# Strassen's seven products for 12 of 32 channel blocks in the two ways out of a retention and pooling trunk

## The chip, the core and the metric

The kernel runs on one core of one Trainium2 chip. The metric is the device time of one execution in microseconds. The engines named below are TensorE (PE, whose weight loads are PEld), VectorE (DVE), ScalarE (ACT), GpSimd (POOL) and SyncE (SP, which issues most of the loads); PSUM is the memory of eight banks into which PE adds its products, each bank 128 partitions by 512 values of fp32.

## What is computed

A trunk of two layers over 256 tokens and 2048 channels. The first is a retention layer of eight heads, the second a gated pooling over four windows; each has a wide way in, its own core, and a way out of 4096 channels back to 2048, which is added to the stream. A last norm ends it.

```python
def retention_layer(x, g_norm, w_in, gn, w_out):
    h = rms_norm(x, g_norm)
    ...
    o = chunkwise_retention(q, k, v)
    ...
    o = o.astype(x.dtype) * jax.nn.silu(z)      # (1, 256, 4096)
    return o @ w_out                            # w_out (4096, 2048)

def pooling_layer(x, g_norm, w_in, w_grp, b_grp, scale, w_out):
    ...
    mix = mix.reshape(B, S, POOL_WIDTH) * scale
    return (mix * jax.nn.silu(z)) @ w_out       # (1, 256, 4096) @ (4096, 2048)

def reference(x, ...):
    h = x
    h = h + retention_layer(h, ...)
    h = h + pooling_layer(h, ...)
    return rms_norm(h, final_norm)
```

## The kernel before

Everything is fp32. A value that goes through PE is held as a pair in the type fp32r: hi, which ACT makes as a cast (`split`, L69), and lo, which DVE makes by subtracting hi from the value (L70). A product of two such pairs is three matmuls: hi by hi, hi by lo, lo by hi.

Weights stream from memory in units of 1 MB, 128 rows by 2048, which SP loads into a ring of three buffers `raw`. `weights` splits each in two halves of 1024 columns into `whi` and `wlo`, three buffers each. So ACT and DVE handle each unit in two instructions of 1024 each, and a `raw` buffer is free again when DVE has done the second.

The way out of layer 1 multiplies `os` (the 256 tokens by 4096 channels, as 32 blocks of 128 channels, each a pair) with `ret_out`. It goes through four column blocks of 512. For each there are two sums in PSUM (`accr`, one for each half of 128 tokens) and eight units; a unit holds four channel blocks of these 512 columns, and each channel block gives three matmuls of 512 columns for each half of the tokens (`row_product`, L334 to L336): 24 matmuls to a unit, 768 in all. Behind each column block DVE adds the two sums to the stream `xn` (L358), ACT squares it for the next norm (L360), and PE transposes it in pieces of 128x128 into `turned` (L366). From there ACT and DVE make `hs2` (`split_scaled`, L74 and L75), the left side of the pool's way in, whose first products are `stationary` (L98, L99). All 16 channel blocks of `hs2` are needed there.

The way out of layer 2 does the same with `gs`, `pool_out` and `accy`, without transposes. In its last column block the last two units are held back, and then done for the first half of the tokens and after that for the second, in an order written by hand (`manual_schedule`), so that the norm of the first half runs while PE does the second. The last unit's pairs have a place of their own, `own`. DVE adds (L478), ACT squares (L480), POOL multiplies by the gain `gb`, DVE works out the root, and the rows are scaled and stored.

What stands ahead of the ways out also counts: `os` is complete when the last head's normalization has gone through its root steps (`rsqrt`, L123 to L139, on `rs_t` and `ors`), its products with the gate `gz` (L322, L325) and a split (L327) into the last four blocks. `gs` is complete behind the last steps of the pool's groups (from L437 on).

A list scheduler orders the instructions of each engine at build time, by a simulated timeline, except where the program asks for its own order. Each engine then works through its list strictly in that order.

## Time and profile before

| | |
|---|---|
| time, median of 3 runs | 1390.14 us (1389.86 to 1391.74) |
| profiled execution, its own time | 1390.88 us |
| span of its trace | 1388.7 us |
| PE busy in the span | 1373.2 us |
| DVE / ACT busy in the span | 958.1 / 681.8 us |
| layer 1's way out, from its first product to its last | 579.4 to 756.4 us |
| layer 2's way out | 1204.6 to 1379.2 us |

Times in the trace are microseconds from the start of the span. The three runs give the time that counts; the profiled execution is one more run, and its trace is what can be read, so a forecast built from rows is first a forecast of 1390.88. A matmul's record is longer than its share of the engine, since matmuls overlap: what one costs where they follow each other is the distance between starts. The tables by stretch give for each stretch its length, then busy time and instructions of PE, PEld, DVE, ACT and POOL, the clock granted to PE as a share of full speed, the share of the DMA engines' time, and GB/s. In a row of a group by line, "out<-in" names what is written and read, with partitions by elements.

### The profile page before, as it was taken

To read this page: it belongs to the slowest core of one execution; us is meant where nothing else is said; L and a number is where in the kernel's file an instruction comes from. 1 tells how busy PE (TensorE), PEld (TensorE's weight loads), DVE (VectorE), ACT (ScalarE), POOL (GpSimd) and SP (SyncE) were. 2 spreads that over 40 slices of the span, in tenths; PEclk is the share of its full clock that TensorE was granted. 3 is DMA by queue.
4 is the path that set the end of the run, shared out by engine and by line. 5 is a ranking of instruction groups with operands and counts; after the bars stand their busy time and mean duration, and the time that the engine had idled before them with its cause. 6 is when DMAs were issued, how large, how long until landed. Compare 5 with 4: busy or idle time off the path is not lost.

```text
span 1388.7 us, 18364 instructions
## 1 busy us (share of the span) xinstructions
PE 1373.2 (99%) x7224; PEld 1177.2 (85%) x7224; DVE 958.1 (69%) x1398; ACT 681.8 (49%) x975; POOL 24.5 (2%) x33
## 2 busy tenths in 40 slices
PE   8999999999999999999999999999999999999997
PEld 7888888888888888888888888888888888888885
DVE  6886868686868676754555767876885896744454
ACT  6554555454545454544444445545454545544443
POOL 0000000000000000000000000000000000000001
PEclk9999999999999999999999999999999999999999
DMA  7545454555554545575555555555555555555552
GB/s 295 182 168 207 165 192 168 187 180 187 181 189 164 185 170 183 180 252 197 191 182 189 180 196 192 188 186 186 195 199 182 185 194 197 210 189 205 184 194 109
DMA packets 39493, 262.66 MB, mean 189 GB/s; under 512 B 4512, under 2 KB 4896, under 8 KB 9072
## 3 DMA queue, kind: packets, MB, share of 16 engines
q1 hardware_dynamic: 37872, 255.93, 52.4%
q0 software_dynamic: 1536, 5.57, 1.1%
q8 instruction: 56, 0.92, 0.3%
q14 instruction: 29, 0.24, 0.0%
HBM read 259.39 MB, written 2.10 MB: 188 GB/s over the span
## 4 chain that ended last, share of the span: by engine, by line
PE 98%; DVE 1%; DMA 1%; ACT 0%; issue 0%; SPq 0%; DVEq 0%; ACTq 0%
PE acc L98 37%; PE acc L99 19%; PE accv L278 4%; PE accv L280 4%; PE accy L334 4%; PE accv L279 4%; PE accr L335 4%; PE accr L336 4%; PE accr L334 4%; PE accy L335 4%; PE accy L336 4%; PE po L298 1%; PE acc L197 1%; DMA xin<-in_xT 1%; PE po L300 1%; PE sc L252 0%
## 5 line engine op out<-in xcount | busy, mean ns | idle before, releaser
L70 DVE TENSOR_TENSOR wlo<-raw,whi 128x1024 fp32r<-128x1024 f32 x470 | 575.3, 1224 | 375.7 <-ACT whi L69 372.6
L69 ACT CAST whi<-raw 128x1024 fp32r<-128x1024 f32 x470 | 494.7, 1053 | 642.4 <-PE acc L98 297.8
L98 PE MATMUL acc<-hs,whi 128*128 128x512 f32 x1984 | 697.3, 395 | 0.0
L99 PE MATMUL acc<-hs,wlo 128*128 128x256 f32 x1984 | 556.3, 281 | 0.0
L98 PEld LDWEIGHTS acc<-hs,whi 128*128 128x128 f32 x1984 | 371.9, 188 | 85.3
L99 PEld LDWEIGHTS acc<-hs,wlo 128*128 128x128 f32 x1984 | 374.9, 189 | 1.1
L335 PE MATMUL accr<-wlo,os 128*128 128x512 f32 x256 | 99.9, 390 | 0.0
L280 PE MATMUL accv<-whi,hs 128*128 128x512 f32 x256 | 99.9, 390 | 0.0
L279 PE MATMUL accv<-wlo,hs 128*128 128x512 f32 x256 | 99.8, 390 | 0.0
L336 PE MATMUL accr<-whi,os 128*128 128x512 f32 x256 | 99.7, 389 | 0.0
L335 PE MATMUL accy<-wlo,gs 128*128 128x512 f32 x248 | 96.5, 389 | 0.0
L336 PE MATMUL accy<-whi,gs 128*128 128x512 f32 x248 | 96.5, 389 | 0.0
L278 PE MATMUL accv<-whi,hs 128*128 128x512 f32 x256 | 92.1, 391 | 0.9 <-DVE qk L108 0.9
L334 PE MATMUL accr<-whi,os 128*128 128x512 f32 x256 | 91.2, 390 | 0.0
L98 PE MATMUL acc<-ms,whi 128*128 128x512 f32 x256 | 90.6, 397 | 0.0
L334 PE MATMUL accy<-whi,gs 128*128 128x512 f32 x248 | 88.1, 389 | 0.0
L99 PE MATMUL acc<-ms,wlo 128*128 128x256 f32 x256 | 72.0, 281 | 0.0
L98 PEld LDWEIGHTS acc<-ms,whi 128*128 128x128 f32 x256 | 48.0, 188 | 11.8
L278 PEld LDWEIGHTS accv<-whi,hs 128*128 128x128 f32 x256 | 48.1, 188 | 11.3 <-DVE qk L108 1.2
L334 PEld LDWEIGHTS accr<-whi,os 128*128 128x128 f32 x256 | 48.1, 188 | 10.0
L336 PEld LDWEIGHTS accr<-whi,os 128*128 128x128 f32 x256 | 48.1, 188 | 9.9
L335 PEld LDWEIGHTS accr<-wlo,os 128*128 128x128 f32 x256 | 48.1, 188 | 9.8
(150 smaller groups left out, 1141.9 us busy)
## 6 DMA issues: line engine op xcount, KB each, us to landing
raw<-in_ret_in SPq DMA_DIRECT2D x92, 1024.0 KB, 4.8
raw<-in_pool_in SPq DMA_DIRECT2D x64, 1024.0 KB, 4.9
raw<-in_ret_out SPq DMA_DIRECT2D x32, 1024.0 KB, 4.9
raw<-in_pool_out SPq DMA_DIRECT2D x32, 1024.0 KB, 4.9
raw<-in_pool_grp SPq DMA_DIRECT2D x16, 1024.0 KB, 4.9
xin<-in_ret_in SPq DMA_DIRECT2D x7, 512.0 KB, 8.3
xn<-in_xN POOLq DMA_DIRECT2D x4, 512.0 KB, 9.3
out<-xn SPq DMA_DIRECT2D x8, 256.0 KB, 2.3
```

Of the source, the lines that this page charges most:

```text
L69: nc.scalar.copy(hi, src)
L70: nc.vector.tensor_tensor(out=lo, in0=src, in1=hi.bitcast(F32), op=ALU.subtract)
L98: nc.tensor.matmul(acc, hi, moving[:, k], start=(k == 0), stop=False)
L99: nc.tensor.matmul(acc[:, :S], lo, moving[:, k, 0], start=False, stop=(k == n - 1))
L197: nc.tensor.matmul(accs[c], hi[:, b], hs[:, k], start=(k == 0), stop=False)
L278: nc.tensor.matmul(accv[t], hs[:, k, 0, ts], hi[:, ws], start=(k == 0), stop=False)
L279: nc.tensor.matmul(accv[t], hs[:, k, 0, ts], lo[:, ws], start=False, stop=False)
L280: nc.tensor.matmul(accv[t], hs[:, k, 1, ts], hi[:, ws], start=False, stop=(k == KT - 1))
L298: nc.tensor.matmul(po[:, :S], vs[:, 0, p, cs], ss[:, q, :S], start=(n == 0), stop=(n == 2))
L334: nc.tensor.matmul(acc, A[:, k, 0, ts], hi, start=first, stop=False)
L335: nc.tensor.matmul(acc, A[:, k, 0, ts], lo, start=False, stop=False)
L336: nc.tensor.matmul(acc, A[:, k, 1, ts], hi, start=False, stop=last)
```

## The change

Strassen's scheme multiplies two 2x2 arrangements of blocks with seven products instead of eight, at the price of sums of blocks ahead of the products and behind them. Here an arrangement is: two halves of 128 tokens by two channel blocks of 128 on the left, two channel blocks by two column blocks of 512 on the right. Of the 32 channel blocks the first 20 go on as before (units "C"), the last 12 form six pairs, block j with block j + 6 (units "S", still 1 MB: two channel blocks by two column blocks). The column blocks are done in two pairs, and a pair of column blocks has 16 units in the order CCCSCSCSCSCSCSCC.

For each pair there are eight sums in PSUM: four of results (c11, c21, c12, c22, by half of the tokens and column block), and p1, p5, p6, p7 for products that go into more than one result. They take all eight banks, so the pools of banks are opened and closed by stage. An S unit needs on DVE three sums of weights (`s0` of 1024, `s1` in two of 512) and the splits of these and of the plain parts: 3.5 times 1024. The left side needs four forms of sums of token blocks, made once for each layer from the last 12 blocks by `sides`: one sum of 128x3072, four of 128x768, four splits. The seven products of an S unit are 21 matmuls. Behind the sixth S, DVE puts p1, p5, p6, p7 and the results together in nine sums out of PSUM (some by way of `u`). The pairs of weights now share one tile `w` with four buffers, hi and lo together; one of four buffers `u0` to `u3` of the pool is dropped, and the weights are laid out in memory in the new order.

```diff
+ORDER = "CCCSCSCSCSCSCSCC"
+NS = ORDER.count("S")
+CLASSIC = ((0, 0), (0, 1), (1, 0), (1, 1), (2, 0), (2, 1), (3, 0), (4, 0), (3, 1), (4, 1))
...
+    def load(src):
         raw = wpool.tile([P, UNIT], F32, tag="raw", name="raw", bufs=3)
         nc.sync.dma_start(out=raw, in_=src)
+        return raw
+    def pair_of(src, n):
+        w = wpool.tile([P, 2, HALF], F32R, tag="w", name="w", bufs=4)
+        hi, lo = w[:, 0, :n], w[:, 1, :n]
+        split(hi, lo, src)
+        return hi, lo
+    def weights(src, own=None):
+        raw = load(src)
         halves = []
         for i in range(2):
+            half = raw[:, i * HALF : (i + 1) * HALF]
             if own is None:
-                hi = wpool.tile([P, HALF], F32R, tag="whi", name="whi")
-                lo = wpool.tile([P, HALF], F32R, tag="wlo", name="wlo")
+                halves.append(pair_of(half, HALF))
             else:
-                hi, lo = own[:, i, 0], own[:, i, 1]
-            split(hi, lo, raw[:, i * HALF : (i + 1) * HALF])
-            halves.append((hi, lo))
+                split(own[:, i, 0], own[:, i, 1], half)
+                halves.append((own[:, i, 0], own[:, i, 1]))
         return halves
...
+    class Sum:
+        def __init__(self, pool, name, n):
+            self.tile, self.n, self.done = pool.tile([P, 512], F32, tag=name, name=name), n, 0
+        def add(self, a_hi, a_lo, w_hi, w_lo):
+            for a, w in ((a_hi, w_hi), (a_hi, w_lo), (a_lo, w_hi)):
+                nc.tensor.matmul(self.tile, a, w, start=(self.done == 0), stop=(self.done == self.n - 1))
+                self.done += 1
+    def sides(A, tmp, pieces):
+        a = tmp[:, : 2 * NS * S].rearrange("p (k s) -> p k s", s=S)
+        s = tmp[:, 2 * NS * S : 2 * NS * S + NS * P].rearrange("p (k s) -> p k s", s=P)
+        blocks = A[:, VT - 2 * NS :]
+        nc.vector.tensor_tensor(out=a, in0=blocks[:, :, 0].bitcast(F32), in1=blocks[:, :, 1].bitcast(F32), op=ALU.add)
+        a11, a21, a12, a22 = a[:, :NS, :P], a[:, :NS, P:], a[:, NS:, :P], a[:, NS:, P:]
+        def put(form, src):
+            for dst, j, n in pieces:
+                split(dst[:, :n, form, 0], dst[:, :n, form, 1], src[:, j : j + n])
+        nc.vector.tensor_tensor(out=s, in0=a21, in1=a22, op=ALU.subtract)
+        put(0, s)
+        nc.vector.tensor_tensor(out=a21, in0=a11, in1=a21, op=ALU.subtract)
+        put(2, a21)
+        nc.vector.tensor_tensor(out=s, in0=s, in1=a11, op=ALU.subtract)
+        put(1, s)
+        nc.vector.tensor_tensor(out=s, in0=s, in1=a12, op=ALU.add)
+        put(3, s)
+        forms = []
+        for dst, j, n in pieces:
+            forms += [[(dst[:, i, m, 0], dst[:, i, m, 1]) for m in range(4)] for i in range(n)]
+        return forms
...
+    def way_out(A, src, forms, pool, order, y, after, own=None):
+        def blk(k, t):
+            ts = slice(t * P, (t + 1) * P)
+            return A[:, k, 0, ts], A[:, k, 1, ts]
+        for p in range(2):
+            plain = sum(1 for k, c in CLASSIC if c == 0) * 12
+            sums = {}
+            for name in order:
+                n = 0 if name == "c22" else 3 * NS
+                sums[name] = Sum(pool, name, n + (plain if name[0] == "c" else 0))
+            out_of = {(t, c): sums[f"c{t + 1}{c + 1}"] for t in range(2) for c in range(2)}
+            classic, strassen, held = iter(CLASSIC), 0, []
+            def add(t, c, op, in1):
+                o = y(t, 2 * p + c)
+                nc.vector.tensor_tensor(out=o, in0=o, in1=in1, op=op)
+            def rows(unit, t):
+                (k4, c), halves = unit
+                for i, (hi, lo) in enumerate(halves):
+                    for j in range(2):
+                        ws = slice(j * 512, (j + 1) * 512)
+                        out_of[t, c].add(*blk(4 * k4 + 2 * i + j, t), hi[:, ws], lo[:, ws])
+            for n, kind in enumerate(ORDER):
+                unit = src[p * len(ORDER) + n]
+                if kind == "C":
+                    last = own is not None and p == 1 and n >= len(ORDER) - 2
+                    u = (next(classic), weights(unit, own if last and n == len(ORDER) - 1 else None))
+                    if last:
+                        held.append(u)
+                    else:
+                        rows(u, 0)
+                        rows(u, 1)
+                    continue
+                raw = load(unit)
+                b = raw.rearrange("p (m f) -> p m f", m=4)
+                s = [wpool.tile([P, 2, 512], F32, tag=f"s{i}", name=f"s{i}", bufs=1) for i in range(2)]
+                nc.vector.tensor_tensor(out=s[0], in0=b[:, 1:3], in1=b[:, None, 0].broadcast_to([P, 2, 512]), op=ALU.add)
+                b_hi, b_lo = pair_of(raw[:, 512:1536], 1024)
+                nc.vector.tensor_tensor(out=s[1][:, 0], in0=s[0][:, 0], in1=b[:, 2], op=ALU.add)
+                nc.vector.tensor_tensor(out=s[1][:, 1], in0=s[1][:, 0], in1=b[:, 3], op=ALU.add)
+                b21 = pair_of(raw[:, 1536:], 512)
+                t_pairs = [pair_of(x.rearrange("p m f -> p (m f)"), 1024) for x in s]
+                def cut(pair, i):
+                    return pair[0][:, i * 512 : (i + 1) * 512], pair[1][:, i * 512 : (i + 1) * 512]
+                k1 = VT - 2 * NS + strassen
+                k2 = k1 + NS
+                s1, s2, s3, s4 = forms[strassen]
+                strassen += 1
+                sums["p1"].add(*blk(k1, 0), *cut((b_hi, b_lo), 0))
+                sums["c12"].add(*s4, *cut((b_hi, b_lo), 1))
+                sums["c11"].add(*blk(k2, 0), *b21)
+                sums["p5"].add(*s1, *cut(t_pairs[0], 0))
+                sums["p7"].add(*s3, *cut(t_pairs[0], 1))
+                sums["p6"].add(*s2, *cut(t_pairs[1], 0))
+                sums["c21"].add(*blk(k2, 1), *cut(t_pairs[1], 1))
+                if strassen == NS:
+                    u = ev.tile([P, 512], F32, tag="u", name="u", bufs=1)
+                    nc.scalar.copy(u, sums["p1"].tile)
+                    add(0, 0, ALU.add, sums["c11"].tile)
+                    add(0, 0, ALU.add, u)
+                    after(0, 2 * p)
+                    nc.vector.tensor_tensor(out=u, in0=u, in1=sums["p6"].tile, op=ALU.add)
+                    add(0, 1, ALU.subtract, u)
+                    add(1, 0, ALU.add, sums["c21"].tile)
+                    nc.vector.tensor_tensor(out=u, in0=u, in1=sums["p7"].tile, op=ALU.add)
+                    add(1, 0, ALU.add, u)
+                    after(1, 2 * p)
+                    add(0, 1, ALU.add, sums["p5"].tile)
+                    add(1, 1, ALU.add, sums["p5"].tile)
+                    add(1, 1, ALU.subtract, u)
+            if held:
+                with tc.manual_schedule(engines={mybir.EngineType.PE}):
+                    for t in range(2):
+                        for u in held:
+                            rows(u, t)
+            for t in range(2):
+                add(t, 1, ALU.add, out_of[t, 1].tile)
+                after(t, 2 * p + 1)
...
+        with tc.tile_pool(name="way1", bufs=1, space=bass.MemoryType.PSUM) as way:
+            tmp = act.tile([P, 2 * NS * S + NS * P], F32, tag="hs", name="tmp")
+            big = pl.tile([P, 4, 4, 2, P], F32R, tag="ms", name="forms")
+            small = pl.tile([P, NS - 4, 4, 2, P], F32R, tag="gz", name="forms")
+            forms = sides(os, tmp, ((big, 0, 4), (small, 4, NS - 4)))
+            hs2 = act.tile([P, KT, 2, S], F32R, tag="hs", name="hs2")
...
+            way_out(os, ret_out, forms, way, ("p1", "p5", "p6", "p7", "c11", "c21", "c12", "c22"), stream, turn)
+        second = ctx.enter_context(ExitStack())
+        second.enter_context(banks("second"))
...
+        with tc.tile_pool(name="way2", bufs=1, space=bass.MemoryType.PSUM) as way:
+            tmp = pl.tile([P, 2 * NS * S + NS * P], F32, tag="ms", name="tmp")
+            forms = act.tile([P, NS, 4, 2, P], F32R, tag="hs", name="forms")
+            forms = sides(gs, tmp, ((forms, 0, NS),))
+            own = pl.tile([P, 2, 2, HALF], F32R, tag="ms", name="own")
+            way_out(gs, pool_out, forms, way, ("p1", "p5", "p6", "c11", "c21", "c12", "c22", "p7"), stream, norm, own)
...
+    def mixed_units(w):
+        w = w.reshape(VT, P, 4, 512)
+        units = []
+        for c in (0, 2):
+            classic, j = iter(CLASSIC), VT - 2 * NS
+            for kind in ORDER:
+                if kind == "C":
+                    k4, i = next(classic)
+                    units.append(w[4 * k4 : 4 * k4 + 4, :, c + i])
+                else:
+                    units.append(np.stack([w[j, :, c + 1], w[j, :, c], w[j + NS, :, c + 1], w[j + NS, :, c]]))
+                    j += 1
+        return np.stack(units).transpose(0, 2, 1, 3).reshape(-1, P, UNIT)
...
-    nc = bacc.Bacc("TRN2", target_bir_lowering=False, num_devices=1)
+    nc = bacc.Bacc("TRN2", target_bir_lowering=False, num_devices=1, dynamic_dma_scratch_size=2048)
```

How this stands in the lists of two engines is shown at three places.

**Layer 1's way out begins, DVE.** Before, the last head's products with the gate `gz` and the split into `os` stand among the subtractions of weights (`wlo`), and nothing else follows from them on this engine:

```order
L322 TENSOR_TENSOR gz_4973<-gz_4973,ors_4952 128x1024
L70 TENSOR_TENSOR wlo_5258<-raw_5251,whi_5257 128x1024
L325 SCALAR_TENSOR_TENSOR gz_4973<-o_4915,vec_73,gz_4973 128x256 x4
L70 TENSOR_TENSOR wlo_5288<-raw_5285,whi_5287 128x1024
L70 TENSOR_TENSOR os_365<-gz_4973,os_365 128x4x256
L70 TENSOR_TENSOR wlo_5292<-raw_5285,whi_5291 128x1024
```

In the changed program the same steps have the subtractions for the first S (`w` from `raw`, from `s0`) between them, and the sum of 3072 behind them:

```order
L346 SCALAR_TENSOR_TENSOR gz_4789<-o_4731,vec_67,gz_4789 128x256 x4
L81 TENSOR_TENSOR w_5135<-raw_5125,w_5135 128x512
L81 TENSOR_TENSOR os_357<-gz_4789,os_357 128x4x256
L81 TENSOR_TENSOR w_5138<-s0_5127,w_5138 128x1024
L369 TENSOR_TENSOR tmp_4996<-os_357 128x3072
```

A few rows on, the first forms stand behind the last split of the first S, the weight sums of the second (`s0`, `s1`) and a plain unit's subtraction; the other forms follow still later:

```order
L81 TENSOR_TENSOR w_5141<-s1_5128,w_5141 128x1024
L433 TENSOR_TENSOR s0_5199<-raw_5197 128x1024
L81 TENSOR_TENSOR w_5167<-raw_5165,w_5167 128x1024
L376 TENSOR_TENSOR tmp_4996<-tmp_4996 128x768
L435 TENSOR_TENSOR s1_5200<-s0_5199,raw_5197 128x512
L378 TENSOR_TENSOR tmp_4996<-tmp_4996 128x6x128
L436 TENSOR_TENSOR s1_5200<-s1_5200,raw_5197 128x512
L81 TENSOR_TENSOR forms_4997<-tmp_4996,forms_4997 128x4x128
L81 TENSOR_TENSOR forms_4998<-tmp_4996,forms_4998 128x2x128
```

What moved: between `os` and the first product that needs a form there is now a list of sums and splits on DVE, with the weights of two S units and of C units among them.

**Layer 1's way out ends, PE.** Before, the pool's products (L98, L99 into `acc`) follow the last product of the way out, and the last transposes come later among them:

```order
L334 MATMUL accr_6079<-whi_6324,os_365 128x512
L335 MATMUL accr_6079<-wlo_6325,os_365 128x512
L336 MATMUL accr_6079<-whi_6324,os_365 128x512
L98 MATMUL acc_6429<-hs2_5178,whi_6421 128x512
L99 MATMUL acc_6429<-hs2_5178,wlo_6422 128x256
L98 MATMUL acc_6429<-hs2_5178,whi_6421 128x512
```

In the changed program, where `turned` has a bank for each quarter and the pool's banks come free with the way out's, the transposes of both last column blocks stand between:

```order
L360 MATMUL c22_5654<-w_6222,os_357 128x512
L360 MATMUL c12_5653<-w_6222,os_357 128x512 x5
L360 MATMUL c22_5654<-w_6222,os_357 128x512 x5
L510 MATMUL turned_6173<-idt_303,xn_4987 128x128
L510 MATMUL turned_6164<-idt_303,xn_4987 128x128 x3
L510 MATMUL turned_6173<-idt_303,xn_4987 128x128 x3
L510 MATMUL turned_6255<-idt_303,xn_4987 128x128
L510 MATMUL turned_6264<-idt_303,xn_4987 128x128
L510 MATMUL turned_6255<-idt_303,xn_4987 128x128 x3
L510 MATMUL turned_6264<-idt_303,xn_4987 128x128 x3
L119 MATMUL acc_6329<-hs2_5020,w_6323 128x512
L120 MATMUL acc_6329<-hs2_5020,w_6323 128x256
```

What moved: the pool's first product (L119, L120) now stands behind 16 transposes, and these behind the sums into `xn`.

**Layer 2's way out ends, DVE.** Before, the subtractions of the last two units stand one after the other, and the first sum out of PSUM comes behind them all:

```order
L70 TENSOR_TENSOR wlo_11674<-raw_11667,whi_11673 128x1024
L70 TENSOR_TENSOR own_10642<-raw_11711,own_10642 128x1024 x2
L70 TENSOR_TENSOR wlo_11704<-raw_11701,whi_11703 128x1024
L70 TENSOR_TENSOR wlo_11708<-raw_11701,whi_11707 128x1024
L478 TENSOR_TENSOR xn_5177<-xn_5177,accy_11495 128x512
L491 TENSOR_SCALAR rs_a_11772<-part_10643,base_10644 128x1
```

In the changed program the two subtractions into `own` and two sums into `xn` stand around the last subtraction of the last S (`w` from `s1`), ahead of the last C but one (`w` from `raw`):

```order
L81 TENSOR_TENSOR w_11478<-s0_11467,w_11478 128x1024
L81 TENSOR_TENSOR own_10406<-raw_11535,own_10406 128x1024
L409 TENSOR_TENSOR xn_4987<-xn_4987,c11_11004 128x512
L81 TENSOR_TENSOR own_10406<-raw_11535,own_10406 128x1024
L81 TENSOR_TENSOR w_11481<-s1_11468,w_11481 128x1024
L409 TENSOR_TENSOR xn_4987<-xn_4987,u_11505 128x512
L81 TENSOR_TENSOR w_11529<-raw_11527,w_11529 128x1024
L81 TENSOR_TENSOR w_11532<-raw_11527,w_11532 128x1024
```

What moved: the first sum out of PSUM, which needs c11 complete, now stands ahead of three subtractions of weights.

## Rows read from the trace of the kernel before

**Rows 1.** Page, part 1 (busy us, share, instructions); the chain by engine

```profile
PE 1373.2 (99%) x7224; PEld 1177.2 (85%) x7224; DVE 958.1 (69%) x1398; ACT 681.8 (49%) x975; POOL 24.5 (2%) x33
...
PE 98%; DVE 1%; DMA 1%; ACT 0%; issue 0%; SPq 0%; DVEq 0%; ACTq 0%
```

**Rows 2.** Waits of PE: who waited <- for whom: us, times, longest

```profile
PE acc L197 <- ACT whi L69: 4.0, 3, 2.4
PE cold L162 <- POOL ones_f L156: 1.0, 1, 1.0
PE accv L278 <- DVE qk L108: 0.9, 1, 0.9
```

**Rows 3.** Both ways out: stretch, busy us (x instructions) by engine, clock, DMA

```profile
579.40:756.40 177.00, 177.00 (x794) 146.54 (x793) 94.90 (x107) 77.77 (x91) 3.39 (x5) 1.00 0.57 203
...
1204.60:1379.20 174.60, 174.52 (x770) 144.04 (x768) 85.18 (x90) 72.64 (x82) 11.74 (x8) 1.00 0.51 175
```

**Rows 4.** Layer 1's sums: duration ns min/median/max, first and last start

```profile
L334 PE MATMUL accr<-whi,os x256: 389/389/476, 579.4 to 755.8; 128*128 128x512 f32 x128
...
L336 PE MATMUL accr<-whi,os x256: 387/389/398, 579.9 to 756.2; 128*128 128x512 f32 x128
```

**Rows 5.** The chain that ended last: start us, us, what

```profile
760.93 0.66 PE turned L366 x6
```

**Rows 6.** DVE in order of time, head 7's end: start us, us, instruction

```profile
579.97 0.43 DVE L138 SCALAR_TENSOR_TENSOR rs_t<-rs_t,rs_a 128x256 f32<-128x256 f32 x1
...
583.52 1.23 DVE L70 TENSOR_TENSOR wlo<-raw,whi 128x1024 fp32r<-128x1024 f32 x1
584.66 0.42 DVE L139 SCALAR_TENSOR_TENSOR ors<-rs_t,ors 128x256 f32<-128x256 f32 x1
585.11 0.42 DVE L137 TENSOR_TENSOR rs_t<-ors 128x256 f32<-128x256 f32 x1
...
592.89 1.23 DVE L70 TENSOR_TENSOR os<-gz,os 128x1024 fp32r<-128x1024 f32 x1
```

**Rows 7.** Groups by line: count, busy us, mean ns, idle before it

```profile
L69 ACT CAST whi<-raw 128x1024 fp32r<-128x1024 f32 x470 | 494.7, 1053 | 642.4 <-PE acc L98 297.8 <-PE accr L336 97.1 <-PE accy L336 88.5
...
L75 DVE SCALAR_TENSOR_TENSOR hs<-turned,vec,hs 128x256 fp32r<-128x256 f32 x16 | 7.1, 477 | 0.1
...
L74 ACT ACTIVATE hs<-turned,vec 128x256 fp32r<-128x256 f32 x16 | 6.8, 471 | 1.7 <-PE turned L366 1.5 <-DVE hs L75 0.2
...
L358 DVE TENSOR_TENSOR xn<-xn,accr 128x512 f32<-128x512 f32 x8 | 5.1, 680 | 0.0
```

**Rows 8.** Instructions of line 210, durations in ns

```profile
L210 DVE TENSOR_TENSOR xin<-xin x3: 685/1218/2293, 28.7 to 34.3; 128x2048 f32<-128x2048 f32 x1, 128x1024 f32<-128x1024 f32 x1, 128x512 f32<-128x512 f32 x1
```

**Rows 9.** DMA issues: count, KB each, median us from issue to landing

```profile
raw<-in_ret_out SPq DMA_DIRECT2D x32, 1024.0 KB, 4.9
```

**Rows 10.** DVE in order of time, layer 2's way out begins

```profile
1204.56 0.48 DVE L437 SCALAR_TENSOR_TENSOR m<-acc,vec,hl 128x256 f32<-128x256 f32 x1
```

**Rows 11.** PE in order of time, layer 1's last product and the next

```profile
756.21 0.39 PE L336 MATMUL accr<-whi,os 128*128 128x512 f32 x1
...
756.44 0.39 PE L98 MATMUL acc<-hs,whi 128*128 128x512 f32 x1
```

**Rows 12.** In order of time, PE's last matmul

```profile
1378.72 0.40 PE L336 MATMUL accy<-own,gs 128*128 128x512 f32 x1
```

**Rows 13.** Stretches at the start and the end, columns as in rows 3

```profile
8.00:10.00 2.00, 1.74 (x7) 1.26 (x5) 0.49 (x1) 0.40 (x2) 0.00 (x0) 0.50 1.00 370
...
14.00:16.00 2.00, 1.64 (x7) 1.11 (x8) 1.71 (x3) 2.00 (x5) 0.00 (x0) 0.96 1.03 400
...
1379.20:1381.20 2.00, 0.00 (x0) 0.00 (x0) 1.08 (x4) 0.98 (x3) 0.46 (x1) 1.00 1.02 384
...
1383.20:1385.20 2.00, 0.00 (x0) 0.00 (x0) 1.20 (x3) 0.57 (x1) 0.00 (x0) 0.50 0.36 137
```

186 lines of the change are left out of this document (79 added, 107 removed).

## The prediction

> **What bounds the kernel now.** I read the engines' totals first, then the chain that ended last, the waits, the stages, and last single rows of the two ways out. PE is busy 99% of the span, and 98% of the chain is PE's [rows 1]. It waits for other engines 4.0 + 1.0 + 0.9 us in all, at the start [rows 2]. In the two ways out (579.4 to 756.4 and 1204.6 to 1379.2 us) PE is busy to within 0.1 us, DVE 54% and 49%, ACT 44% and 42% [rows 3]. So each product taken away is worth its whole pitch, as long as every product left finds its operands ready. In layer 1's way out 768 products start between 579.4 and 756.2 [rows 4], with 24 transposes of 0.11 (six take 0.66 us [rows 5]) among them: (176.8 - 2.6) / 767 = 0.227 us each.
>
> **What it removes.** 12 of 32 blocks are six pairs; per pair and half of the columns seven products of three matmuls stand where there were eight: 3 matmuls less, 6 x 2 x 2 x 3 = 72 in all. 72 x 0.227 = **16.3 us less**. Loads stay at 1 MB per unit.
>
> **What it adds, in the steady part.** A Strassen unit (S) brings DVE two sums of 1024 in width (three instructions) and 3.5 subtractions of 1024 where a plain unit (C) has two. A row of 1024 at 583.52 takes 1.23 us, and the next starts at 584.66: 1.14 after it [rows 6]; with the same overlap 0.68 at 512 [rows 7] gives 0.60, and 0.42 at 256 gives 0.34, while rows of 256 that need the row ahead stand 0.45 apart [rows 6]. From 2293 ns at 2048 and 1218 at 1024 [rows 8], 768 takes 0.87 and 3072 3.3 us. A pair S + C then costs DVE 3.5 x 1.14 + 2 x 1.14 + 2.34 = 8.6 us and PE (21 + 24) x 0.227 = 10.2. ACT has 5.5 casts of 1.05 [rows 7]: 5.8. All of it lies beside PE, and I cost it at nothing. One loop is tight: a raw block is loaded when the second subtraction of the C ahead ends, 4.9 us from issue to landing [rows 9]; then the sum, the last subtraction of the S under way, the next C's two and half a sum (4 x 1.14 + 0.6) must pass until it is free again: about 10.1 against 10.2. After an entry (below) the operands of the next C are some 2.6 us early, so I take 0 here, and at most 4 us in all if two loads meet and land 0.5 us later.
>
> **The entry of layer 1.** S reads four forms made from the last 12 blocks of os, and the last four blocks are written by head 7's end, 592.89 + 1.23 in the rows [rows 6]. PE meanwhile has three C, and the changed order lets it draw C4 ahead: 72 + 24 + 21 = 117 matmuls, 26.6 us, from 579.4 to 606.0. DVE must in the same time get from the first S's sum to the fourth form. I carry its queue in the changed order. The head's first root step stands at 579.97 + 0.43 [rows 6]; in the changed order two rows of the last gate block (0.34 each) and a wait for its copy come ahead of it: 581.4. The raw block for the sum lands at 581.6 (its buffer is free once C1's second half is subtracted, by the same carry 576.6, plus 4.9). Up to the first piece of the fourth form stand 12 rows of 1024 (13.7 us), 9 of 512 (5.4), 14 of 256 (5.3), 4 of 768 (3.5), one of 3072 (3.3), memsets (0.3): 31.5 us. Three waits for ACT's casts come to 1.8: the os cast, one for the cast of C4's second half (whose pair comes free only when PE has done the third form's products) and the fourth form's. 581.6 + 31.5 + 1.8 = 614.9, visible at 615.1. Behind it PE has one matmul and 12 more of C4: 618.1. **Loss 12.1 us.** DVE is then 85% loaded, PE is the bound again, and nothing gives this back.
>
> **The entry of layer 2.** The same with 120 matmuls (1204.6 + 27.2 = 1231.8). DVE is at the last but one block's bias step at 1204.56 [rows 10]; 12 rows of 1024 (13.7), 5 of 512 (3.0), 8 of 768 (7.0), 3.3, and the pool's last six steps (2.7) end at 1234.4; 13 matmuls follow: 1237.4. **Loss 5.6 us**; it is smaller because no head's end stands in the queue.
>
> Here a rule can be weighed. The two rows at 583.52 and 584.66 overlap by 0.09 us [rows 6]. The Trainium skill ("VectorE: DVE Perf Modes", Terms) says that a pipeline flush follows every DVE operation and that the next can't issue until the pipe is empty; by that, without any overlap, some 70 rows would add about 6 us to the two losses. The row decides, and I use the pitches.
>
> **The turn between the layers.** Before, PE goes on at 756.44 with the pool's products, 0.23 us after the last one [rows 11], and turns the last columns among them. In the changed order all 16 transposes stand ahead of the pool's first product, and on DVE the last sum (c22) stands behind a split of the third column's turned block. From the last product: 0.8 (seven transposes), ACT 0.47, DVE 0.48, the sum 0.68 [rows 7], six transposes 0.66, with releases 3.35 us, where 15 transposes alone take 1.65. **Loss 1.7 us.**
>
> **The end of layer 2.** Ahead of the last S's fourth subtraction stand own's two and the first sum out of PSUM, which waits for c11. From the end of the C before: c11 visible at 1.75 (7 matmuls and 0.16), sum 2.35, own 3.5, subtraction done 4.7; PE is there after 16 matmuls, 3.6. Then a sum (0.6) and 1.14 stand ahead of the next half: 6.4 against 5.7. **Loss 1.9 us.** The nine sums out of PSUM that follow end 4 us before PE does, so the 9.6 us from the end of PE's last matmul (1378.72 + 0.40 [rows 12]) to the end of the span stay.
>
> **The clock.** In layer 1's entry PE has from about 597.4 to 602.3 one matmul, and up to 614.4 works a third of the time. After PE's last matmul the granted clock is 1.00 from 1379.2 to 1381.2 and 0.50 (1.2 GHz) from 1383.2 to 1385.2; at the start it is 0.50 from 8 to 10, with PE 87% busy, and 0.96 from 14 to 16 [rows 13]. A fall can cost nothing (DVE is the bound there), or half of some 6 us once PE runs free: 0 to 3. I take 2, nearer to the rows of the start.
>
> **Sum.** -16.3 + 12.1 + 5.6 + 1.7 + 1.9 + 2.0 = +7.0. The profiled execution took 1390.88 (span 1388.7 and 2.2 around it): 1397.9. The median of three is 0.74 lower: **1397 us, slower**.
>
> **Rivals.**
> The entries are hidden. Half of the subtractions and sums for the first S need weights only; were they done beside the head's last products, the forms would come earlier. For: DVE is 54% busy over the way out before [rows 3]. Against: only four pairs of buffers, and in the queue the head's root steps stand among them. With both entries hidden: 1390.1 - 16.3 + 3.6 = 1377; with half of the losses, 1386 to 1390. It decides for faster once the four losses together are under 13.5 us.
> More waits than counted. The raw block's loop above (up to 4), and the clock. The Trainium skill ("TensorE: Matmul & The Clock Gate", Part 1) says that the throttled state is the default and that activity releases it. By that, where the rows only show that idling to the end brings 0.50, the thin activity of the entry could already do so; the price in rows is the whole 3. Time: 1399 to 1404. For: the loop has 0.1 us of room. Against: margins after the entries.
> That the change doesn't do what it says I give nothing: the built program has 72 matmuls less.
>
> **How the numbers follow.** About 0.2% (2.8 us) is what a measurement here can tell from no change. Forecast, 1393 to 1399: 0.55. More waits: 0.2. Entries half hidden, 1387 to 1393: 0.13; hidden further, below 1387: 0.12. So faster 0.12, same 0.13, slower 0.75. The range 1387 to 1403 leaves out the hidden entries and the far end of the waits.
>
> **What would show it.** After: PE waiting in layer 1's way out about 12 us, nearly all in its first 40, for DVE's subtractions of forms and weights; about 5.6 in layer 2's first 35; 1 to 2 at the turn, for xn; 2 in the last 25 us; none in between; 72 matmuls less at 0.227. DVE near 95% in the entries and 85% after. A granted clock under 1 between 600 and 622 shows the clock's term. I am wrong if PE waits under 8 us in layer 1's way out, or if S + C pairs take more than 10.3 us.

## The result, and the profile after

| | before | after |
|---|---|---|
| time, median | 1390.06 us (1389.86 to 1391.74, 4 runs) | 1401.51 us (1401.20 to 1403.37, 4 runs) |
| profiled execution, span | 1390.88, 1388.7 us | 1403.37, 1401.4 us |
| ratio of the runs | | 1.0082, interval 1.0065 to 1.0100 |

The change makes the kernel 11.4 us slower. The forecast was 1397, within 1387 to 1403: direction and range held, and the loss was 1.6 times the 7.0 of the sum. The traced execution of after is the slowest of its four, 1.9 us above the median; its first head's products start at 36.25 us, in the trace of before at 35.38.

The page of after, as in [rows 1]: instructions and busy time of the engines, and the chain by engine. PE has 72 matmuls less, DVE is busy 143 us more, and PE's share of the chain falls from 98% to 92%.

```profile
PE 1367.8 (98%) x7152; PEld 1167.2 (83%) x7152; DVE 1101.6 (79%) x1571; ACT 735.4 (52%) x1039; POOL 24.4 (2%) x33
...
PE 92%; DVE 4%; DMA 2%; ACT 1%; issue 1%; SPq 0%; DVEq 0%; ACTq 0%
```

The waits of PE, as in [rows 2] (who waited <- for whom: us, times, longest). None of these six was there before.

```profile
PE c L360 <- DVE w L81: 4.6, 3, 2.6
...
PE acc L119 <- DVE rs_t L158: 3.0, 1, 3.0
PE c L360 <- ACT w L80: 2.7, 3, 1.2
PE turned L510 <- DVE xn L409: 2.6, 2, 2.3
...
PE c L360 <- DVE m L585: 1.0, 1, 1.0
...
PE c L360 <- DVE gz L129: 0.9, 1, 0.9
```

The stretches, with the columns of [rows 3]: the first 41 us of layer 1's way out and the rest of it, then the same for layer 2.

```profile
576.90:618.00 41.10, 34.15 (x129) 24.98 (x130) 37.33 (x54) 17.96 (x24) 3.40 (x5) 0.92 0.52 175
618.00:761.00 143.00, 141.83 (x631) 115.73 (x629) 123.19 (x137) 81.05 (x101) 0.00 (x0) 1.00 0.56 201
...
1216.70:1250.00 33.30, 31.45 (x133) 24.65 (x134) 30.12 (x31) 17.10 (x20) 0.53 (x1) 1.00 0.52 189
1250.00:1385.00 135.00, 133.16 (x575) 108.07 (x574) 117.97 (x125) 71.82 (x83) 7.49 (x5) 0.99 0.50 180
```

By the last or first matmul of each stage, in us:

| stage | before | after | difference |
|---|---|---|---|
| start to the first product of layer 1's way out | 579.4 | 576.9 | -2.5 |
| from there to the pool's first product | 177.0 | 189.4 | +12.4 |
| from there to the first product of layer 2's way out | 448.2 | 450.4 | +2.2 |
| from there to the end of PE's last matmul | 174.5 | 174.5 | 0.0 |
| behind it | 9.6 | 10.2 | +0.6 |

Each way out has 36 matmuls less, 8.2 us. So layer 1 lost 20.6 us between its first product and the pool's, layer 2 8.2 us, and the stretch ahead of layer 1 gained 2.5 although the diff does nothing there that the sum had priced.

### The profile page after: what moved, and what is told of

It reads as the page before. It is cut to its first block, busy times and chain, and to the rows that moved or that the text cites. A ratio compares the mean times of both kernels' runs of the same rounds, so it can differ in the third digit from the quotient of the medians.

```text
span 1401.4 us, 18352 instructions
## 1 busy us (share of the span) xinstructions
PE 1367.8 (98%) x7152; PEld 1167.2 (83%) x7152; DVE 1101.6 (79%) x1571; ACT 735.4 (52%) x1039; POOL 24.4 (2%) x33
## 4 chain that ended last, share of the span: by engine, by line
PE 92%; DVE 4%; DMA 2%; ACT 1%; issue 1%; SPq 0%; DVEq 0%; ACTq 0%
PE acc L119 37%; PE acc L120 19%; PE c L360 16%; PE accv L300 4%; PE accv L301 4%; PE accv L299 4%; PE p L360 4%; DVE w L81 2%; DMA raw<-in_pool_out 1%; PE acc L218 1%; PE po L319 1%; PE po L321 1%; DMA xin<-in_xT 1%; DVE xn L409 1%; PE acc L219 1%
## 5 line engine op out<-in xcount | busy, mean ns | idle before, releaser
L119 PE MATMUL acc<-hs,w 128*128 128x512 f32 x1984 | 694.5, 393 | 3.0 <-DVE rs_t L158 3.0
L81 DVE TENSOR_TENSOR w<-raw,w 128x1024 fp32r<-128x1024 f32 x470 | 560.3, 1199 | 134.4 <-ACT w L80 127.4
L80 ACT CAST w<-raw 128x1024 fp32r<-128x1024 f32 x470 | 480.1, 1030 | 267.9 <-PE acc L120 74.3
L120 PE MATMUL acc<-hs,w 128*128 128x256 f32 x1984 | 556.6, 281 | 0.0
L119 PEld LDWEIGHTS acc<-hs,w 128*128 128x128 f32 x1984 | 372.4, 188 | 85.7 <-issue 3.2
L120 PEld LDWEIGHTS acc<-hs,w 128*128 128x128 f32 x1984 | 375.7, 189 | 1.0
L360 PE MATMUL c<-w,os 128*128 128x512 f32 x552 | 137.5, 395 | 6.9 <-DVE w L81 4.0
L360 PE MATMUL c<-w,gs 128*128 128x512 f32 x528 | 130.3, 394 | 2.4 <-DVE m L585 1.0
L360 PEld LDWEIGHTS c<-w,os 128*128 128x128 f32 x552 | 103.5, 189 | 31.8 <-DVE w L81 5.3
L360 PEld LDWEIGHTS c<-w,gs 128*128 128x128 f32 x528 | 99.6, 190 | 25.4 <-DVE w L81 2.1
L301 PE MATMUL accv<-w,hs 128*128 128x512 f32 x256 | 99.9, 390 | 0.0
L300 PE MATMUL accv<-w,hs 128*128 128x512 f32 x256 | 99.8, 390 | 0.0
L299 PE MATMUL accv<-w,hs 128*128 128x512 f32 x256 | 97.2, 390 | 0.0
L119 PE MATMUL acc<-ms,w 128*128 128x512 f32 x256 | 90.6, 397 | 0.0
L120 PE MATMUL acc<-ms,w 128*128 128x256 f32 x256 | 72.0, 281 | 0.0
L119 PEld LDWEIGHTS acc<-ms,w 128*128 128x128 f32 x256 | 48.1, 188 | 11.8
L301 PEld LDWEIGHTS accv<-w,hs 128*128 128x128 f32 x256 | 48.0, 188 | 10.1
```

Source lines behind the costliest of these rows:

```text
L80: nc.scalar.copy(hi, src)
L81: nc.vector.tensor_tensor(out=lo, in0=src, in1=hi.bitcast(F32), op=ALU.subtract)
L119: nc.tensor.matmul(acc, hi, moving[:, k], start=(k == 0), stop=False)
L120: nc.tensor.matmul(acc[:, :S], lo, moving[:, k, 0], start=False, stop=(k == n - 1))
L299: nc.tensor.matmul(accv[t], hs[:, k, 0, ts], hi[:, ws], start=(k == 0), stop=False)
L300: nc.tensor.matmul(accv[t], hs[:, k, 0, ts], lo[:, ws], start=False, stop=False)
```

## Where the losses lie in the trace of after

For this I set each matmul of the ways out at its pitch (0.227 us from start to start, a transpose 0.11) and added up by how much PE's starts fell behind that.

**Layer 1's entry: 12.0 us** from 576.9 to 612.7. DVE, in order of time (start us, us, instruction):

```profile
577.80 1.23 DVE L433 TENSOR_TENSOR s<-raw 128x1024 f32<-128x1024 f32 x1
...
594.48 3.35 DVE L369 TENSOR_TENSOR tmp<-os 128x3072 f32<-128x3072 f32 x1
...
607.75 1.23 DVE L81 TENSOR_TENSOR w<-raw,w 128x1024 fp32r<-128x1024 f32 x1 [0.76 <-ACT w L80]
...
611.59 1.03 DVE L81 TENSOR_TENSOR forms<-tmp,forms 128x512 fp32r<-128x512 f32 x2 [0.69 <-ACT forms L80]
```

The first S's sum starts at 577.8, the fourth form ends at 612.6. DVE is busy 37.33 of the 41.10 us; in the 19.3 us up to 612.7 PE starts 33 matmuls, which are 7.5 us at their pitch. PE's idle time in the whole stretch is 41.10 - 34.15 = 6.95 us; the other 5 of the 12.0 are matmuls at a slower pace while PE waits on DVE's list anyway. Two stretches of the entry and two behind the turn show the clock (columns as above, the clock third from the end; 0.50 is 1.2 GHz, 1.00 is 2.4 GHz, and 0.69 is a mean over both):

```profile
597.00:608.00 11.00, 6.30 (x14) 3.75 (x14) 10.24 (x19) 3.19 (x6) 0.00 (x1) 0.69 0.50 161
608.00:613.00 5.00, 4.04 (x14) 2.23 (x14) 4.05 (x7) 2.56 (x6) 0.00 (x0) 1.00 0.56 202
...
766.00:768.00 2.00, 1.72 (x5) 1.55 (x6) 1.49 (x9) 0.27 (x1) 0.00 (x0) 0.50 0.00 0
768.00:770.00 2.00, 2.00 (x7) 1.66 (x7) 0.42 (x1) 0.14 (x1) 0.00 (x0) 0.50 0.00 0
```

**The turn: 7.85 us** between the last product's end at 758.43 and the pool's first. Before there is nothing between the two: they start 0.23 us apart, one pitch [rows 11]. First PE, then DVE, in order of time:

```profile
758.46 0.93 PE L510 MATMUL turned<-idt,xn 128*128 128x128 f32 x7
759.71 0.44 PE L510 MATMUL turned<-idt,xn 128*128 128x128 f32 x2 [0.32 <-DVE xn L409]
762.44 0.87 PE L510 MATMUL turned<-idt,xn 128*128 128x128 f32 x6 [2.29 <-DVE xn L409]
766.28 0.76 PE L119 MATMUL acc<-hs,w 128*128 128x512 f32 x1 [2.97 <-DVE rs_t L158]
```

```profile
757.84 1.22 DVE L81 TENSOR_TENSOR w<-raw,w 128x1024 fp32r<-128x1024 f32 x1
...
760.17 1.22 DVE L81 TENSOR_TENSOR w<-raw,w 128x1024 fp32r<-128x1024 f32 x1
...
761.70 0.68 DVE L409 TENSOR_TENSOR xn<-xn,c 128x512 f32<-128x512 f32 x1
...
765.66 0.48 DVE L86 SCALAR_TENSOR_TENSOR hs<-turned,vec,hs 128x256 fp32r<-128x256 f32 x1
```

Behind a subtraction DVE has two sums into `xn` to do, then a subtraction of the pool's weights, then c22 at 761.70; only then can PE turn the last column. And the pool's first product starts when DVE's last split of `hs2` has ended (765.66 + 0.48), though it needs the first block alone; the profile puts its release down to a step of the norm (`rs_t`) that ends just behind that split. The clock falls meanwhile, and the pool runs at 0.50 until 770: 1.8 us more, by the first eleven matmuls.

Between the entry and the turn PE is never idle, but 1.5 us are lost in its pace: before, nearly all matmuls of this way out stand 0.226 or 0.227 us apart, and in after, from 620 to 757, about four in ten stand 0.231 to 0.236 apart.

**Layer 2's entry: 1.0 + 3.1 us.** PE waits 1.0 for the pool's bias step (`m`) ahead of its first product, and loses 3.1 up to 1244.

**Layer 2's end: 4.6 us** from 1372 on. ACT, then PE:

```profile
1372.17 2.00 ACT L80 CAST own<-raw 128x1024 fp32r<-128x1024 f32 x2 [2.62 <-DMA raw<-in_pool_out]
1374.08 1.04 ACT L80 CAST w<-s 128x1024 fp32r<-128x1024 f32 x1
```

```profile
1375.17 0.50 PE L360 MATMUL p<-w,forms 128*128 128x512 f32 x1 [0.82 <-ACT w L80]
...
1376.60 0.50 PE L360 MATMUL c<-w,gs 128*128 128x512 f32 x1 [0.70 <-ACT w L80]
```

ACT waits 2.62 us for the last unit's block to land, casts it into `own`, and the last S's `s1`, whose product PE waits for, is cast only behind that. By then the blocks of the S units land late as well; DVE's first sums of the last two S units:

```profile
1351.76 1.23 DVE L433 TENSOR_TENSOR s<-raw 128x1024 f32<-128x1024 f32 x1 [1.83 <-DMA raw<-in_pool_out]
...
1362.08 1.23 DVE L433 TENSOR_TENSOR s<-raw 128x1024 f32<-128x1024 f32 x1 [1.58 <-DMA raw<-in_pool_out]
```

They start 10.3 us apart and each waits for its block. PE hardly waits for these two units; it is the cast into `own`, in front of one that PE needs, that hands such a wait on to it. The clock falls here too:

```profile
1378.00:1380.00 2.00, 2.00 (x5) 1.13 (x5) 2.00 (x2) 0.71 (x2) 1.21 (x1) 0.50 0.00 0
1380.00:1382.00 2.00, 2.00 (x7) 1.57 (x7) 2.00 (x3) 0.00 (x0) 0.22 (x1) 0.70 0.00 0
```

At 0.50 the starts stand 0.43 apart, and some 1.5 of the 4.6 us are matmuls at that pace. DVE is busy throughout, so how much of the 1.5 a full clock would have given back isn't shown.

## The experiments

Each ran beside the kernel before on its chip; times are medians, ratios against the kernel before. That kernel took 1390.0 to 1391.0 us on these chips, so a difference from after of under 1 us tells nothing.

**Layer 1's entry: is it the length of DVE's list?** The forms of layer 1 are left out, and plain blocks of `os` stand in their place, so the sums are not those of the reference.

```diff
-            forms = sides(os, tmp, ((big, 0, 4), (small, 4, NS - 4)))
+            forms = [
+                [(os[:, k, 0, ts : ts + P], os[:, k, 1, ts : ts + P]) for k in (n, n + NS) for ts in (0, P)]
+                for n in range(VT - 2 * NS, VT - NS)
+            ]
```

> The changed kernel, layer 1 alone: the four forms of the left side are not made (the sum of 3072, the four of 768 and the splits are left out, and plain blocks of os stand in their place, so the result is another one). Products, weights and sums out of PSUM stay. Theory: layer 1's entry costs 12 us because DVE's list is long, and of that list the forms are 12 us: the entry's loss falls to 0 to 2 us and the time to 1389.5 (1388 to 1392). Rival: the wait is for the last head's blocks of os or for weights, which stay: 1397 or more.

Measured: 1394.49 us, 7.0 less than after; neither theory's number. By stage the answer is clear. The stretches of layer 1's entry, and the eleven us in which the clock had been 0.69:

```profile
576.30:617.40 41.10, 40.87 (x179) 33.54 (x180) 36.51 (x51) 21.18 (x24) 3.40 (x5) 1.00 0.67 234
597.00:608.00 11.00, 11.00 (x50) 9.10 (x49) 8.53 (x10) 6.51 (x7) 0.00 (x0) 1.00 0.94 337
```

PE is busy 40.87 of 41.10 us, and the clock stays at 1.00; the way out is 12.7 us shorter (168.8 against 181.5). The 5.2 us that are missing in the total lie in the pool, 455.6 us instead of 450.4, where the change does nothing: its pairs of matmuls run there at 0.3533 us each throughout, in after from about 870 on at 0.3467 (on this pitch see the last section). So the theory holds for its place: DVE's list is the entry's loss, and without the forms' share of it next to nothing is lost (0.6 us).

**The turn: does the closing of the PSUM pools force the order?**

```diff
-    def banks(name):
...
+    psum = [
+        ctx.enter_context(tc.tile_pool(name="ps_acc", bufs=3, space=bass.MemoryType.PSUM)),
+        ctx.enter_context(tc.tile_pool(name="ps_ret", bufs=5, space=bass.MemoryType.PSUM)),
+    ]
+    def bank(i, name):
+        ret = i < 5
+        return psum[ret].tile([P, 512], F32, tag="ret" if ret else "acc", name=name)
...
-                    turned = way.tile([P, 512], F32, tag=(("p1", "p5"), ("p6", "p7"))[c % 2][i], name="turned")
+                    turned = bank(0, "turned")
```

> The changed kernel, but the PSUM banks stay one set for the whole program (three and five buffers in rotation, as in the kernel before) instead of pools that are closed and opened at each way out, so that the pool's first products wait only for their own bank and the last transposes can go among them. In the changed kernel 7.85 us lie between the last product of layer 1's way out and the pool's first. Theory: 5 of them come from the order that the closed pool forces (all transposes and all splits of hs2 first): 1396.5 us (1395 to 1398). Rival: DVE's list of sums and splits sets the turn in either order, and the pool's products wait for hs2 instead of for the bank: 1400 or more.

Measured: 1394.52 us (1.0028, 1.0019 to 1.0038), 7.0 less than after. PE at the turn, in order of time:

```profile
755.62 0.39 PE L118 MATMUL acc<-hs,w 128*128 128x512 f32 x1
755.85 2.43 PE L359 MATMUL c<-w,os 128*128 128x512 f32 x10
758.11 0.28 PE L119 MATMUL acc<-hs,w 128*128 128x256 f32 x1
...
760.70 1.04 PE L509 MATMUL turned<-idt,xn 128*128 128x128 f32 x8
```

A product of the pool now runs even inside the way out, and the transposes go among the pool's products without idle time. DVE is no faster: its last sum starts at 760.74, 2.9 us behind the start of PE's last product of the way out (757.89), but PE now has other products to do. The waits for `gz` (0.9) and `m` (1.0), ahead of the two ways out, are gone as well: they too were waits for a pool of banks to close, as was most of the turn. These 1.9 us fit the 2 us that it brought beyond the theory. Layer 1's entry, which this edit leaves as it was, still loses 13.4 us.

**Layer 2's end: ACT's wait or DVE's list?** On the kernel with one set of banks, `own` goes to the last unit but one.

```diff
-                    u = (next(classic), weights(unit, own if last and n == len(ORDER) - 1 else None))
+                    u = (next(classic), weights(unit, own if last and n == len(ORDER) - 2 else None))
```

> The kernel with one set of PSUM banks (1394.5 us), with the place of its own (own) given to the last unit but one instead of the last. In the changed kernel ACT waits 2.62 us for the last unit's block to land before it casts it, and the last sums of weights of the last S stand behind that cast; with the earlier unit the block lands one unit earlier. Theory, the loss of about 4.6 us at layer 2's end comes mostly from this wait in ACT's list: it falls to about 2, 1392 us (1391 to 1393.5). Rival, it comes from DVE's list (two subtractions into own and the sums out of PSUM ahead of the subtractions that PE needs), which stays: 1394 or more.

Measured: 1389.23 us (0.9990, 0.9981 to 0.9999), 5.3 less. ACT in order of time:

```profile
1354.51 2.00 ACT L79 CAST own<-raw 128x1024 fp32r<-128x1024 f32 x2 [0.22 <-DMA raw<-in_pool_out]
```

It waits 0.22 for the block instead of 2.62, and PE loses 0.3 us there instead of 5.1. The theory holds, and for more than it said (it expected 1391 to 1393.5): the whole of the loss goes, since ACT's wait had passed on to DVE's list behind it.

**Can POOL take the sums of weights?**

```diff
-                nc.vector.tensor_tensor(out=s[0], ...)
-                nc.vector.tensor_tensor(out=s[1][:, 0], ...)
-                nc.vector.tensor_tensor(out=s[1][:, 1], ...)
+                nc.gpsimd.tensor_tensor(out=s[0], ...)
+                nc.gpsimd.tensor_tensor(out=s[1][:, 0], ...)
+                nc.gpsimd.tensor_tensor(out=s[1][:, 1], ...)
```

> The changed kernel with one edit: the three sums of weights of an S unit (one of 1024, two of 512) run on POOL instead of DVE. From POOL's row of 128x512 in the changed kernel (1.42 us) they take about 5.7 us per unit there, beside 10.2 us of PE for an S and a C. Theory that DVE's list sets both entries: two units' sums leave the list of layer 1's entry (2 x 2.34 us), one or two that of layer 2's, and the loop of a raw block gets shorter: 1394.5 us (1392 to 1397). Rival: POOL's sums are too slow for the first S units, or slow DVE down beside them, and hold the raw blocks longer: 1401 or more.

Measured: 1428.00 us, 26.5 more than after. Groups by line, of after and then of this kernel:

```profile
L81 DVE TENSOR_TENSOR w<-raw,w 128x1024 fp32r<-128x1024 f32 x446 | 544.5, 1227 | 133.1 <-ACT w L80 126.2
```

```profile
L81 DVE TENSOR_TENSOR w<-raw,w 128x1024 fp32r<-128x1024 f32 x446 | 622.8, 1406 | 132.9 <-ACT w L80 125.6
...
L433 POOL TENSOR_TENSOR s<-raw 128x1024 f32<-128x1024 f32 x24 | 71.3, 2970 | 467.4 <-DMA raw<-in_ret_out 219.3 <-ACT gs L80 173.6 <-DVE w L81 42.9
```

The rival held, with a price for which it had no number: the 446 subtractions took 1406 ns in the mean instead of 1227, 78 us of DVE's time more; POOL's sums of 1024 took 2970. DVE was spared 24 x 2.34 = 56 us and lost more than that: it is busy 1145.0 us, against 1101.6. The same row in the pool (800 to 1200 us), where POOL has no sums to do, and then in layer 1's way out (620 to 760 us):

```profile
L81 DVE TENSOR_TENSOR w<-raw,w 128x1024 fp32r<-128x1024 f32 x144 | 176.3, 1224 | 40.5 <-ACT w L80 37.3
```

```profile
L81 DVE TENSOR_TENSOR w<-raw,w 128x1024 fp32r<-128x1024 f32 x39 | 82.1, 2143 | 2.7 <-ACT w L80 2.4
```

The Trainium skill ("SBUF — State Buffer", "SBUF: two separate sides") says that DVE and GpSimd share a pair of ports, and that one of them is fully blocked while the other holds it, for DVE instructions with two SBUF inputs too. These rows agree in direction; they do not show who held what when, nor how much of the 26.5 us is the slow subtractions and how much POOL's own pace.

**Would more plain units ahead of the first S cover the entry?** On one set of banks, with orders of their own for the two pairs of columns (the plain units are put in a fitting order with it):

```diff
-ORDER = "CCCSCSCSCSCSCSCC"
+ORDERS = ("CCCCCSCSCSCSCSCS", "CCSCSCSCSCSCSCCC")
```

> The kernel with one set of PSUM banks (1394.5 us) and other orders of units: five C ahead of the first S in the first pair of columns (CCCCCSCSCSCSCSCS), and the S units of the second pair earlier (CCSCSCSCSCSCSCCC), so that three C stand at each layer's end. Theory: layer 1's entry loss falls from 12 to about 7 us (PE has 10.9 us more to do, DVE's list grows by 4.6), layer 2's from 4 to about 0, the loss at layer 2's end from 5 to about 1, because the last unit's block no longer has to land ahead of the last S: 1383 us (1381 to 1387). Rival: the loss only moves, since DVE's list grows with each C put ahead and S units stand closer to the joint between the two pairs of columns: 1391 or more.

Measured: 1396.30 us (1.0039), no better than with the banks alone. The rival held. The entries do lose less, 8.3 us in layer 1 and nothing in layer 2, but at the joint between the pairs of columns PE now loses about 7 us in each layer. DVE and PE there, in layer 2:

```profile
1292.70 1.23 DVE L436 TENSOR_TENSOR s<-raw 128x1024 f32<-128x1024 f32 x1 [2.12 <-DMA raw<-in_pool_out]
```

```profile
1295.12 5.74 PE L362 MATMUL c<-w,gs 128*128 128x512 f32 x24 [2.77 <-DVE w L83]
```

In layer 2 the S units stand so close at the joint that a raw block is late (2.12 us), and the nine sums out of PSUM stand among the subtractions. In layer 1 part of the loss stands ahead of a transpose (2.4 us), for which the profile names no cause. With POOL's sums in addition:

> Both of the two kernels before it together: one set of banks, the other orders, and the sums of weights on POOL. Theory: layer 1's entry loss falls to about 3 us, the rest stays as with the orders: 1379 us (1376 to 1383). Rival (POOL's sums slow or late): no gain over the orders alone, or a loss.

Measured: 1416.14 us, 19.8 more than without; the rival again, and the 446 subtractions take 1410 ns in the mean.

**Fewer pairs, so that there are plain units enough.** With four pairs, 24 blocks stay plain, and each long list of DVE gets its cover.

```diff
-ORDER = "CCCSCSCSCSCSCSCC"
+ORDERS = ("CCCCCCSCSCSCSCCC", "CCCSCSCSCSCCCCCC")
```

> Four pairs instead of six (24 of 32 channel blocks plain), one set of PSUM banks, and orders with more C where DVE's list is long: CCCCCCSCSCSCSCCC and CCCSCSCSCSCCCCCC, so six C ahead of the first S, six at the joint of the two pairs of columns, six at the end. 48 matmuls less than before instead of 72: 10.9 us. Theory: with the joint pairs of weights alone the kernel before takes 1385.9; of the 10.9 us further the entries give back 1 to 2, the joint and the turn 1 to 2, the end 1 to 2: 1379.5 us (1376.5 to 1383). Rival: the loss moves once more, as with the orders for six pairs: 1386 or more.

Measured: 1377.09 us, 0.9903 of the kernel before (0.9887 to 0.9920): 13 us faster than before and 24 faster than after. The first stretch of each way out:

```profile
575.50:616.60 41.10, 41.10 (x183) 33.94 (x182) 38.92 (x56) 20.89 (x25) 3.40 (x5) 1.00 0.64 229
...
1196.20:1229.50 33.30, 33.30 (x149) 27.55 (x148) 24.31 (x29) 15.34 (x19) 0.53 (x1) 1.00 0.67 238
```

PE has no idle time in either. It beats both kernels with two thirds of the saving. Not all of the 13 us is Strassen's: the joint pairs of weights alone take the kernel before to 1385.9 us (the next experiment). Against that, four pairs bring about 8.8 of their 10.9 us, so some 2 are given back. Fewer pairs, the orders and the one set of banks came in together here; what each is worth wasn't measured.

**Why are the heads faster?** The way out of layer 1 begins 2.5 us earlier in after. First, the kernel before with hi and lo of a weight in one tile (the same edit stands in layer 1's way in, not shown):

```diff
-                hi = wpool.tile([P, HALF], F32R, tag="whi", name="whi")
-                lo = wpool.tile([P, HALF], F32R, tag="wlo", name="wlo")
+                w = wpool.tile([P, 2, HALF], F32R, tag="w", name="w", bufs=3)
+                hi, lo = w[:, 0], w[:, 1]
```

> The kernel before, with one edit: the hi and lo half of a split weight lie in one tile of 128 x 2 x 1024 (still three of them) instead of two tiles. In the trace of the changed kernel each of the seven later heads is 0.71 us shorter (70.12 against 70.83), which the prediction did not have, 4 to 5 us in all. Theory: it comes from where hi and lo lie, so this kernel takes about 1385.5 us (1384 to 1387). Rival: it comes from something else in the change (the fourth pair, the smaller DMA scratch that moves all other tiles, the order of the instructions): 1390, within 1 us of the kernel before.

Measured: 1385.86 us (0.9968, 0.9957 to 0.9980). The first term of layer 1's way out now starts at 575.8, in [rows 4] at 579.4 (duration min/median/max, first and last start):

```profile
L334 PE MATMUL accr<-w,os x256: 389/389/476, 575.8 to 752.2; 128*128 128x512 f32 x128
```

So that part of the change alone is worth some 4 us: 4.7 beside the kernel before on its chip (1390.59), 3.6 in the traces, all of it ahead of layer 1's way out. The opposite edit, on after (two tiles, four buffers each, in `pair_of` and in layer 1's way in):

> The changed kernel with hi and lo in tiles of their own again (four of each). Theory that the place of hi and lo shortens the heads: 1406 us (1405 to 1407), 4.5 more than the changed kernel's 1401.5. Rival, something else shortens them: 1401.5, within 1 us.

Measured: 1407.99 us, 6.5 more than after, 2 more than the theory. Waits of PE:

```profile
PE c L360 <- DVE m L585: 4.8, 1, 4.8
PE c L360 <- DVE gz L129: 4.5, 1, 4.5
```

By the traces layer 1's way out begins 6.6 us later (583.5 against 576.9). Of this 3.6 us are the longer wait for `gz`, which was 0.9 in after, and 3.0 lie ahead of it, where the heads are slower, as said. The wait for `m`, 1.0 in after, grows by 3.8. Against this the ways out are 4.0 and 1.9 us shorter. So the total is no clean price of the joint pairs. The two waits are the ones that vanish with one set of banks. What else of the change could do it:

> The kernel before with the DMA scratch of 2048 of the changed kernel and nothing else, so that tiles may lie elsewhere. Theory: the heads' pitch hangs on how hi and lo lie to each other, which stays: 1390, within 1 us of the kernel before. Rival: it hangs on where everything lies: 1386 or another time more than 2 us away.

> The same with four buffers each for hi and lo in tiles of their own, as in the kernel with pairs apart (whose layer 1 way out began at 583.5 us, against 579.4 in the kernel before and 576.9 in the changed one). Theory, the distance of hi and lo decides (16 KB per partition instead of 12): the heads take 4 us more, 1394 us (1393 to 1395). Rival, that kernel's heads were slower for the order of its instructions: 1390, within 1 us.

> The same with joint pairs, four of them, and the small scratch: all that the change does to the weights, without Strassen. Theory: 1385.9 us as with three joint pairs (1385 to 1387), since PE is not waiting for pairs in the kernel before. Rival: the fourth pair brings or costs over 1 us.

Measured: 1390.67 (1.0002, 0.9993 to 1.0012), 1390.54 (1.0001, 0.9991 to 1.0010) and 1385.90 us (0.9967, 0.9954 to 0.9980). The small scratch does nothing, four pairs instead of three do nothing. My theory that the distance of hi and lo decides, so that four buffers apart would cost 4 us, fell. In the heads joint or apart is what counts; why, stays open.

## Why the prediction was right, and where its terms were off

| term | predicted | in the trace of after |
|---|---|---|
| 72 matmuls | -16.3 | -16.3 |
| S and C by turns | 0 to 4, taken 0 | 1.5 in layer 1, 0.3 in layer 2 |
| layer 1's entry | +12.1 | +12.0, and 0.9 ahead of it |
| the clock in that entry | +2.0 | under 0.8 by my reading, and that within the 12.0 |
| layer 2's entry | +5.6 | +3.1, and 1.0 ahead of it |
| the turn | +1.7 | +6.2 (7.85 less the 1.65 of the transposes), 1.8 by the clock behind it |
| layer 2's end | +1.9 | +4.6, and 0.6 behind it |
| joint pairs | not seen | about -4 |
| start of the run | 0 | +0.9 |

The right column adds up to 12.6 us; the spans differ by 12.7. The range held, but the forecast's own bracket, 1393 to 1399, did not: the turn and layer 2's end cost 7.2 us more than their terms, and the joint pairs, which no term had, gave 4 of that back. That part is luck.

- **The saving** is there to the matmul (7224 to 7152 on the page), and PE was the bound, so it counted in full. Right.
- **The steady part.** Pairs of S and C follow each other in 10.34 us in layer 1 and 10.20 in layer 2, where 10.2 was said; DVE is 86% busy there (123.19 of 143.00), where 85% was said. The 10.34 is just past the 10.3 that the prediction named as a sign of being wrong. Yet PE doesn't wait between entry and turn; its own matmuls stand farther apart, as shown above, so in these pairs it is PE's pace, and not the loop of a raw block, that makes the time. What sets this pace stays open. At layer 2's end the loop took 10.3 us where 10.1 was said, so its 0.1 us of room was gone there.
- **Layer 1's entry.** The loss is right to 0.1. The mechanism is as said: that the list is the cause, the kernel without forms shows. That the number is so close is luck: the first sum came at 577.8 (581.6 was said) and the last form at 612.6 (614.9), so the list took 34.8 us instead of 33.3, and PE began 2.5 us earlier; these three cancel. The prediction's sign, that PE waits 12 us there, holds for the time lost; idle time alone is 6.95, which is under the 8 that it named as a sign of being wrong, so the sign was not put sharply enough.
- **The clock.** It fell as the rival feared (0.69 in those eleven us), with PE only 57% busy, and cost little by my reading: DVE's subtraction waits 0.76 us for a cast behind the slow matmuls, and I find nothing else of it on the path. No run has the same list at a full clock, so this is argued and not shown; the kernel without forms doesn't have the fall. The Trainium skill ("TensorE: Matmul & The Clock Gate", Part 1) has the rule that was weighed, that throttled is the default; these rows agree with it. The price of 3 us that the prediction set beside the rule was not paid. The clock took 1.8 us at the turn, and up to 1.5 at layer 2's end, where the prediction had none.
- **Layer 2's entry** was over-sized: DVE's list cost 3.1 us instead of 5.6. The 1.0 ahead of it is a wait for banks, of which the prediction had nothing.
- **The turn** is the term that failed most. The step said that one split stands ahead of c22 and that the transposes follow. In the trace DVE is 3.3 us behind at PE's last product, because the nine sums out of PSUM stand in the same list as the pool's first weights, and the pool's first product waits for the last split of `hs2`. The prediction knew that all transposes stand ahead of that product; it didn't ask what the product itself waits for when the banks' pool is closed and a new one opened. Two more such waits, 0.9 and 1.0, came from the same thing. With one set of banks all of it is gone.
- **Layer 2's end** was looked for on DVE (the right rows, two subtractions into `own` and a sum), and its trigger was on ACT: a cast that waits for a block, ahead of one that PE needs. The prediction carried DVE's list there, not ACT's. The loop of a raw block, which runs without room there, was in the prediction, as a rival.
- **The rivals.** "More waits than counted" (0.2) has the measured time in its 1399 to 1404, but of its two mechanisms the clock gave a part, and the raw loop came only by way of ACT's list. "The entries are hidden" was wrong for this kernel and is what four pairs with six plain units ahead achieve.
- **What was missed** are the 4 us of the joint pairs, a gain; with pairs apart the changed kernel takes 1408, outside the range (longer waits for banks are in that number too). The prediction gave that edit no term.

## What to carry to other kernels

In this kernel fewer products were worth their pitch only where every list that feeds them had work of the bound engine to hide behind: six pairs saved 16.3 us and gave back more than that, four pairs saved 10.9 and kept about 8.8. Where a pool of PSUM banks is closed between stages, ask what the first product of the next stage waits for, since it can be the last reader of the old banks rather than its operand. In a strict list, look for the instruction that waits for a load and stands ahead of one that is needed: moving one unit's buffer was worth 5.3 us.
